# Gate and up projections of a decoder layer: two of eight pairs of channel tiles by seven products of block sums, some low parts by accumulating transfers

## The chip, the cores and the metric

The kernel runs on one core of a Trainium2 chip. The metric is device time in microseconds (us) of one execution; lower is better. The engines of the core are named as in the profile: PE multiplies matrices (PEld is its loading of the stationary operand), DVE and ACT work element by element, POOL does little arithmetic here and issues software DMA transfers, SP issues the weight loads.

## What is computed

One decoder layer over 256 tokens of 2048 channels: a normalised input projection, three branches (windowed attention, pooling, a state-space mixer), an output projection, and a feed-forward part, in which the change lies. All of it is float32.

```
h2 = rmsnorm(x, ln2_w)
gu = h2 @ w_gate_up                     # 2048 x 11264: 5632 gate columns, then 5632 up columns
x = x + (silu(gu[..., :D_FF]) * gu[..., D_FF:]) @ w_down
return rmsnorm(x, final_w)
```

## The kernel before

PE multiplies float32 in a reduced form, so each operand is split in two: `hi`, the value rounded by a cast, and `lo`, what the cast lost. A product is then three matmuls (`three`): x_hi by w_hi, x_hi by w_lo, x_lo by w_hi. The activations are split once. The weights are split as they stream in: `weights` loads 1 MB of a weight matrix (`raw`, 4 channel tiles of 128 rows by 512 columns, on SP's queue) and makes two pieces of it, each of 2 channel tiles, 128 partitions by 1024 elements. For each, `split` has ACT cast `whi` from `raw` and then DVE subtract, `wlo = raw - whi`. There are four buffers of `raw` and five each of `whi` and `wlo`, so that a piece can be made only when the products of the fifth piece before it are done.

The feed-forward part takes the 5632 columns in 11 blocks of 512 (FB = 11), in three parts of 4, 4 and 3 blocks (FF_PARTS), numbered 0 to 10. For a block, `tokens_block` makes the gate (16 channel tiles, 2 tiles of tokens, three matmuls of 128x512 each: 96 matmuls) and then the up projection (96 more), each into two of the four PSUM banks of `acc`. ACT puts the gate through Silu (L871), DVE multiplies the up projection by it (L877). The result `ff` has tokens on its partitions and is wanted with channels there: `turn` makes 16 small transposes on DVE (L342, tile `tt`) and then splits `tt` into `f_hi` (ACT) and `f_lo` (DVE). After each part the down projection takes those `f` tiles as its activations.

The code does not write out the order on each engine. A scheduler sorts the instructions by the order of the program and by what they depend on; each engine then runs its own list strictly in order. `turn` does not run where it is called: it puts its pieces in a list (`later`), and the products call `side` behind each piece of weights, which takes the next entry from that list. So the 16 transposes of a block stand among the weight pieces of the block after it.

Lines of before that the text names: L139 and L140 (the two halves of `split`), L200 to L202 (`three`), L342 (`turn`), L618 (a transfer `mt` of an earlier stage, issued by POOL), L857 (the sum behind the down projection), L862, L871, L877. The same code has other numbers after the change: the split is L142 and L143, `three` is L211 to L213, the transposes are L460.

Of the kernel before, what the change touches and what calls it, by code (L numbers as in the profile page):

```python
# [71 lines left out]
def hybrid_block(ctx: ExitStack, tc: tile.TileContext, ins, out):  # L72
# [6 lines left out]
    small = ctx.enter_context(tc.tile_pool(name="small", bufs=1))  # L79
    dram = ctx.enter_context(tc.tile_pool(name="dram", bufs=1, space=bass.MemoryType.DRAM))  # L80
# [11 lines left out]
    def k1(shape, dt=F32, name="k1", tag="k1", bufs=6):  # L92
        return work.tile([P, *shape], dt, tag=tag, name=name, bufs=bufs)
# [51 lines left out]
    def weights(loads, shape):  # L145

        raw = wpool.tile([P, *shape], F32, tag="raw", name="raw", bufs=4)
        for to, src in loads:
            sp.dma_start(to(raw), src)
        n, cols = shape  # L150
        parts = []
        for h in range(2):
            a, b = h * (n // 2), (h + 1) * (n // 2)
            hi = wpool.tile([P, b - a, cols], F32R, tag="whi", name="whi", bufs=5)
            lo = wpool.tile([P, b - a, cols], F32R, tag="wlo", name="wlo", bufs=5)
            split(raw[:, a:b], hi, lo)
# [264 lines left out]
    v = work.tile([P, T, 256], F32, tag="v", name="v", bufs=1)  # L421
# [220 lines left out]
    bnat = k2([GROUPS, P], F32, "bnat", "bnat", 1)  # L642
# [184 lines left out]


# [19 lines left out]
    fw = [k1([256], F32, "fw", "tk", 16) for _ in range(8)]  # L848
# [16 lines left out]

    for some in FF_PARTS:
        f = Parts(4 * len(some), "f")
        for i, b in enumerate(some):
            a_ = k4([T, NB], F32, "ff")
            for t, a in enumerate(tokens_block(x2p, KD, plain_loads(wgu, 0, b * NB, NB), NB)):  # L870
                act.activation(a_[:, t, :], a, AF.Silu, scale=rstd2[:, t:t + 1])  # L871
# [76 lines left out]
```

## Time and profile before

| | |
|---|---|
| median of 3 runs | 1663.43 us (1662.54 to 1664.08) |
| the profiled execution | 1662.15 us |
| its span, from the first to the last instruction | 1660.4 us |
| what lies around the span | 1.75 us |
| PE busy | 1645.3 us, 99% of the span |
| DVE busy | 1139.6 us, 69% |
| ACT busy | 825.2 us, 50% |
| POOL busy | 65.9 us, 4% |
| mean granted clock of PE | 0.998 of full speed |

An engine is busy, in this table, while it has an instruction in work. Matmuls overlap, so PE's share says only that it nearly always had one in work; the distance between the starts of two matmuls says how fast they pass. A wait is put down to the instruction that released it.

### The profile page before, as it was taken

What the parts mean: (1) busy time and instruction counts of PE and PEld (TensorE: products, weight loads), DVE (VectorE), ACT (ScalarE), POOL (GpSimd) and SP (SyncE); (2) the same over time, 40 slices, a digit from 0 to 9 for tenths busy, and PEclk for the clock granted to TensorE, in tenths of its full rate; (3) what the DMA queues carried; (4) which work ended last, traced back from release to release, by engine and by line L of the source; (5) the groups of instructions that cost most, each with busy time, mean ns of one, the idle gap of its engine ahead of it and who ended that gap; (6) DMA issues with size and microseconds to landing.
All of it is one profiled execution on the core that took longest, in us unless ns stands there. A gap on an engine that the chain in (4) does not pass through costs nothing.

```text
span 1660.4 us, 20066 instructions
## 1 busy us (share of the span) xinstructions
PE 1645.3 (99%) x7815; PEld 1373.5 (83%) x7815; DVE 1139.6 (69%) x1592; ACT 825.2 (50%) x1071; POOL 65.9 (4%) x62
## 2 busy tenths in 40 slices
PE   9999999999999999999999999999999999999997
PEld 8888888888888888888788888888888888888887
DVE  7689898955654569844898866665556666446675
ACT  6467678544444456644445544443344444344443
POOL 1000001200300000000000000000000000000000
PEclk9999999999999999999999999999999999999999
DMA  9654665455566555655575565556655655655552
GB/s 298 185 174 142 186 203 190 171 182 181 189 204 195 187 171 183 228 196 184 178 253 190 186 202 184 183 191 210 201 178 203 202 186 195 201 184 198 194 173 89
DMA packets 185647, 316.68 MB, mean 191 GB/s; under 512 B 7532, under 2 KB 57968, under 8 KB 185552
## 3 DMA queue, kind: packets, MB, share of 16 engines
q1 hardware_dynamic: 183856, 310.67, 56.6%
q0 software_dynamic: 1552, 4.66, 0.9%
q8 instruction: 61, 1.00, 0.2%
q14 instruction: 34, 0.28, 0.0%
q10 hardware_dynamic: 144, 0.07, 0.0%
HBM read 313.25 MB, written 2.13 MB: 190 GB/s over the span
## 4 chain that ended last, share of the span: by engine, by line
PE 94%; DVE 3%; ACT 1%; DMA 1%; issue 0%; POOLq 0%; SPq 0%; POOL 0%; DVEq 0%; ACTq 0%
PE acc L202 26%; PE acc L200 26%; PE acc L201 26%; PE acc L238 9%; PE acc L239 5%; DVE tt L342 2%; DVE wlo L140 1%; PE sm L675 1%; DMA x<-in_x_dram 1%; PE tr L524 0%; ACT whi L139 0%; PE sm L567 0%; PE tr L556 0%; PE sm L682 0%; PE sm L688 0%
## 5 line engine op out<-in xcount | busy, mean ns | idle before, releaser
L140 DVE TENSOR_TENSOR wlo<-raw,whi 128x1024 fp32r<-128x1024 f32 (+2 forms) x582 | 704.6, 1226 | 440.3 <-ACT whi L139 438.6
L139 ACT CAST whi<-raw 128x1024 fp32r<-128x1024 f32 (+2 forms) x582 | 605.5, 1044 | 664.8 <-PE acc L202 595.5
L200 PE MATMUL acc<-whi,x2p_hi 128*128 128x512 f32 x704 | 273.9, 389 | 0.0
L201 PE MATMUL acc<-wlo,x2p_hi 128*128 128x512 f32 x704 | 273.9, 389 | 0.0
L202 PE MATMUL acc<-whi,x2p_lo 128*128 128x512 f32 x704 | 273.9, 389 | 0.0
L238 PE MATMUL acc<-h,whi 128*128 128x512 f32 x672 | 238.4, 398 | 0.0
L200 PE MATMUL acc<-whi,h 128*128 128x512 f32 (+1 forms) x544 | 211.4, 389 | 1.8 <-ACT h L142 1.0
L202 PE MATMUL acc<-whi,h 128*128 128x512 f32 (+1 forms) x544 | 208.6, 385 | 0.3
L201 PE MATMUL acc<-wlo,h 128*128 128x512 f32 (+1 forms) x544 | 208.7, 384 | 0.0
L239 PE MATMUL acc<-h,wlo 128*128 128x256 f32 x672 | 189.0, 282 | 0.0
L201 PEld LDWEIGHTS acc<-wlo,x2p_hi 128*128 128x128 f32 x704 | 132.1, 188 | 27.5
L200 PEld LDWEIGHTS acc<-whi,x2p_hi 128*128 128x128 f32 x704 | 132.1, 188 | 27.4
L202 PEld LDWEIGHTS acc<-whi,x2p_lo 128*128 128x128 f32 x704 | 132.1, 188 | 27.4
L238 PEld LDWEIGHTS acc<-h,whi 128*128 128x128 f32 x672 | 126.0, 188 | 30.3 <-issue 1.8
L202 PE MATMUL acc<-whi,f_lo 128*128 128x512 f32 (+1 forms) x352 | 134.5, 382 | 0.4 <-DVE f_lo L140 0.4
L200 PE MATMUL acc<-whi,f_hi 128*128 128x512 f32 (+1 forms) x352 | 134.4, 382 | 0.0
L201 PE MATMUL acc<-wlo,f_hi 128*128 128x512 f32 (+1 forms) x352 | 134.4, 382 | 0.0
L239 PEld LDWEIGHTS acc<-h,wlo 128*128 128x128 f32 x672 | 126.9, 189 | 1.9 <-issue 1.8
L200 PEld LDWEIGHTS acc<-whi,h 128*128 128x128 f32 x544 | 102.3, 188 | 23.5 <-issue 2.3
L202 PEld LDWEIGHTS acc<-whi,h 128*128 128x128 f32 x544 | 101.9, 188 | 21.2 <-DVE h L143 0.7
L201 PEld LDWEIGHTS acc<-wlo,h 128*128 128x128 f32 x544 | 102.2, 188 | 20.8 <-issue 0.7
L342 DVE STREAM_TRANSPOSE tt<-ff 32x256 f32<-32x256 f32 x176 | 76.7, 436 | 2.7
(238 smaller groups left out, 1744.1 us busy)
## 6 DMA issues: line engine op xcount, KB each, us to landing
raw<-in_w_in_dram SPq DMA_DIRECT2D x106, 1024.0 KB, 5.2
raw<-in_w_gate_up_dram SPq DMA_DIRECT2D x88, 1024.0 KB, 5.1
raw<-in_w_down_dram SPq DMA_DIRECT2D x43, 1024.0 KB, 5.1
raw<-in_w_ssm_br_dram SPq DMA_DIRECT2D x16, 1024.0 KB, 5.1
raw<-in_w_out_dram SPq DMA_DIRECT2D x16, 1024.0 KB, 6.2
raw<-in_w_attn_br_dram SPq DMA_DIRECT2D x8, 1024.0 KB, 5.1
raw<-in_w_pool_br_dram SPq DMA_DIRECT2D x8, 1024.0 KB, 5.0
x<-in_x_dram SPq DMA_DIRECT2D x8, 512.0 KB, 7.9
```

The lines of the kernel that those rows point to most:

```text
L139: act.copy(hi, src)
L140: dve.tensor_tensor(lo, src, hi.bitcast(F32), ALU.subtract)
L200: pe.matmul(o, lhsT=xh, rhs=yh, start=first, stop=False)
L201: pe.matmul(o, lhsT=xh, rhs=yl, start=False, stop=False)
L202: pe.matmul(o, lhsT=xl, rhs=yh, start=False, stop=last)
L238: pe.matmul(accs[c], lhsT=hi[:, j, cols], rhs=a.both(k), start=k == 0, stop=False)
L239: pe.matmul(accs[c][:, :SEQ], lhsT=lo[:, j, cols], rhs=a.hi(k), start=False, stop=k == KD - 1)
L342: dve.transpose(to[32 * j:32 * j + 32, :, :, i, :], src[32 * i:32 * i + 32, :, :, j, :])
L675: pe.matmul(p[:, i * HD:(i + 1) * HD], lhsT=mt[:, i, :], rhs=xdt[:, i, :], start=True, stop=True)
```

## The change

Gate and up of a block are made together, by `two_blocks`, which uses all eight PSUM banks at once: four of `acc` (q1, q7, q5, q6), two of `tr` (q2, q4) and two of `sm` (q3, q8). The 16 channel tiles form eight pairs. For a pair, the activations are two tiles of tokens by two channel tiles, and the weights two channel tiles by two blocks of columns (gate and up): a product of 2 by 2 blocks. Pairs 0 and 1 (`forms`) make it from seven products of sums of blocks, the others from eight products of blocks. The pairs go in the order 0, 2, 1, 3, 4, 5, 6, 7.

- The sums on the activation side are made once (`block_forms`, on DVE). Those on the weight side are made in every block (`block_weights`): `vu` (two blocks), then one sum into `raw` (L278), then another (L279), all on DVE, and each is split. Such a pair has three pieces of two tiles and one of one tile (`shi`, `slo`). Call the three A (the two gate blocks as loaded), B (`vu`) and C (the two later sums): pair 0 makes A, B, C and pair 1 makes A', B', C'. Pair 2 between them has the pieces D and E.
- After pair 1 four merges put sums of the products together (L324 to L328): `s1` by ACT from PSUM, `u2`, `u3`, `s5` and `u2` again by DVE. Behind the last pair DVE adds these to the banks q2, q4 (L994) and q3, q8 (L1001); Silu and the multiplication (L995, L1002) then work on SBUF.
- Pairs 3 and 6 (`by_dma`) get the low part of their weights in another way: ACT writes `lo = -raw` (L161), a transfer issued by POOL (L162) takes `raw` from SBUF and adds it onto `lo` in SBUF (512 KB, accumulating), and ACT casts `hi` (L165). DVE does nothing for these pairs. There are four such transfers in a block, 44 in all. Pair 3's two pieces are called F and G here. `side` is called with 1.8 times the share behind such a piece.
- `raw` has three buffers instead of four; a raw tile of gate and up is filled by two loads of 512 KB. Small tiles of the early stages go to a pool that is closed before this stage.

The core of the diff:

```
-    def weights(loads, shape):
-
-        raw = wpool.tile([P, *shape], F32, tag="raw", name="raw", bufs=4)
+    def weights(loads, shape, by_dma=False):
+        raw = wpool.tile([P, *shape], F32, tag="raw", name="raw", bufs=3)
         for to, src in loads:
             sp.dma_start(to(raw), src)
         n, cols = shape
@@ -153,7 +157,14 @@
             a, b = h * (n // 2), (h + 1) * (n // 2)
             hi = wpool.tile([P, b - a, cols], F32R, tag="whi", name="whi", bufs=5)
             lo = wpool.tile([P, b - a, cols], F32R, tag="wlo", name="wlo", bufs=5)
-            split(raw[:, a:b], hi, lo)
+            if by_dma:
+                act.activation(lo, raw[:, a:b], AF.Copy, scale=-1.0)
+                pool.dma_start(
+                    lo.rearrange("p a c -> p (a c)"), raw[:, a:b].rearrange("p a c -> p (a c)"), accum_op=ALU.add
+                )
+                act.copy(hi, raw[:, a:b])
+            else:
+                split(raw[:, a:b], hi, lo)
             parts.append((a, b, hi, lo))
         return parts
...
+    def block_weights(w, k, c1, c2):
+        raw = wpool.tile([P, 4, NB], F32, tag="raw", name="raw", bufs=3)
+        for j, c in enumerate((c1, c2)):
+            sp.dma_start(raw[:, 2 * j:2 * j + 2, :], rows(w, k, 2, c, NB))
+        vu = wpool.tile([P, 2, NB], F32, tag="vu", name="vu", bufs=2)
+        out = []
+        def part(src):
+            hi = wpool.tile([P, 2, NB], F32R, tag="whi", name="whi", bufs=5)
+            lo = wpool.tile([P, 2, NB], F32R, tag="wlo", name="wlo", bufs=5)
+            split(src, hi, lo)
+            out.extend((hi[:, i], lo[:, i]) for i in range(2))
+        part(raw[:, 0:2])
+        dve.tensor_tensor(vu, raw[:, 0::3], raw[:, 2:3].broadcast_to([P, 2, NB]), ALU.add)
+        part(vu)
+        dve.tensor_tensor(raw[:, 2], vu[:, 0], raw[:, 3], ALU.add)
+        dve.tensor_tensor(raw[:, 0], raw[:, 2], raw[:, 1], ALU.add)
+        part(raw[:, 0::2])
+        hi = late.tile([P, NB], F32R, tag="shi", name="shi", bufs=3)
+        lo = late.tile([P, NB], F32R, tag="slo", name="slo", bufs=3)
+        split(raw[:, 3], hi, lo)
+        out.append((hi, lo))
+        return out
+    def two_blocks(a, forms, w, c1, c2, nk, by_dma=()):
+        q1, q7, q5, q6 = acc(), acc(), acc(), acc()
+        q2, q4, q3, q8 = tr(), tr(), sm(), sm()
+        seven = sorted(forms)
+        plain = [p for p in range(nk // 2) if p not in forms]
+        order = []
+        for i, p in enumerate(seven):
+            order += [p] + plain[i:i + 1]
+        order += plain[len(seven):]
+        for p in order:
+            ka, kb = 2 * p, 2 * p + 1
+            if p in forms:
+                f = forms[p]
+                b11, b21, v, u, z, w_, b22 = block_weights(w, ka, c1, c2)
+                first, last = p == seven[0], p == seven[-1]
+                tok = [slice(t * P, (t + 1) * P) for t in range(T)]
+                def form(i):
+                    return f[:, 0, i], f[:, 1, i]
+                def tile_(k, t):
+                    return a.hi(k)[:, tok[t]], a.lo(k)[:, tok[t]]
+                for q, x, y, ends in (
+                    (q1, tile_(ka, 0), b11, True),
+                    (q7, form(3), u, True),
+                    (q5, form(1), v, True),
+                    (q6, form(2), w_, True),
+                    (q2, tile_(kb, 0), b21, False),
+                    (q4, tile_(kb, 1), z, False),
+                    (q3, form(0), b22, False),
+                ):
+                    three(q, *x, *y, first, last and ends)
+                if last:
+                    s1, u2, u3, s5 = (k2([NB], F32, n) for n in ("s1", "u2", "u3", "s5"))
+                    act.copy(s1, q1)
+                    dve.tensor_tensor(u2, q6, s1, ALU.add)
+                    dve.tensor_tensor(u3, q7, u2, ALU.add)
+                    dve.tensor_tensor(s5, q5, u2, ALU.subtract)
+                    dve.tensor_tensor(u2, q5, u3, ALU.subtract)
+            else:
+                by = p in by_dma
+                loads = [
+                    ((lambda r, j=j: r[:, 2 * j:2 * j + 2, :]), rows(w, ka, 2, c, NB)) for j, c in enumerate((c1, c2))
+                ]
+                for j, (_, _, hi, lo) in enumerate(weights(loads, [4, NB], by)):
+                    for t in range(T):
+                        q = ((q2, q4), (q3, q8))[j][t]
+                        for k in range(2):
+                            xh, xl = a.hi(ka + k)[:, t * P:(t + 1) * P], a.lo(ka + k)[:, t * P:(t + 1) * P]
+                            three(
+                                q, xh, xl, hi[:, k], lo[:, k],
+                                q is q8 and p == plain[0] and k == 0, p == plain[-1] and k == 1,
+                            )
+                    side((1.8 if by else 1.0) * 1024 * SHARE)
+        return ((q2, s1), (q4, u3)), ((q3, s5), (q8, u2))
...
+    forms = block_forms(x2p, (0, 1))
     for some in FF_PARTS:
         f = Parts(4 * len(some), "f")
         for i, b in enumerate(some):
             a_ = k4([T, NB], F32, "ff")
-            for t, a in enumerate(tokens_block(x2p, KD, plain_loads(wgu, 0, b * NB, NB), NB)):
-                act.activation(a_[:, t, :], a, AF.Silu, scale=rstd2[:, t:t + 1])
+            gates, ups = two_blocks(x2p, forms, wgu, b * NB, DFF + b * NB, KD, by_dma=(3, 6))
+            for t, (q, more) in enumerate(gates):
+                dve.tensor_tensor(a_[:, t, :], q, more, ALU.add)
+                act.activation(a_[:, t, :], a_[:, t, :], AF.Silu, scale=rstd2[:, t:t + 1])
             if b == FB - 1:
                 act.activation(tiny([1], "junk1"), a_[:, 1, :1], AF.Square)
                 act.activation(tiny([1], "junk1"), rstd2[:, :1], AF.Sqrt)
-            for t, a in enumerate(tokens_block(x2p, KD, plain_loads(wgu, 0, DFF + b * NB, NB), NB)):
+            for t, (q, more) in enumerate(ups):
+                dve.tensor_tensor(more, q, more, ALU.add)
                 dve.scalar_tensor_tensor(
-                    a_[:, t, :], a, rstd2[:, t:t + 1], a_[:, t, :], ALU.mult, ALU.mult
+                    a_[:, t, :], more, rstd2[:, t:t + 1], a_[:, t, :], ALU.mult, ALU.mult
                 )
             turn(a_, 4 * i, f)
         k0, nk = 4 * some[0], 4 * len(some)
```

What this moves is shown at the border between two blocks. First DVE before the change: `raw_8473` is the last weight tile of a block, `raw_8509` the first of the block behind it.

```order
L140 TENSOR_TENSOR wlo_8476<-raw_8473,whi_8475 128x1024
L140 TENSOR_TENSOR wlo_8480<-raw_8473,whi_8479 128x1024
L877 SCALAR_TENSOR_TENSOR ff_8120<-acc_8279,rs2_r_7781,ff_8120 128x512
L877 SCALAR_TENSOR_TENSOR ff_8120<-acc_8280,rs2_r_7781,ff_8120 128x512
L342 STREAM_TRANSPOSE tt_8419<-ff_8120 32x2x4x32 x16
L140 TENSOR_TENSOR wlo_8512<-raw_8509,whi_8511 128x1024
L140 TENSOR_TENSOR wlo_8516<-raw_8509,whi_8515 128x1024
L140 TENSOR_TENSOR f_lo_7809<-tt_8419,f_hi_7808 128x1024
```

The transposes are followed by two pieces of weights and then by `f_lo`. Next, DVE after the change: `ff_8543` is the result of a block. `raw_8943` (pieces D and E) and `raw_8994` (A', B' and C', with `whi_8998`, `whi_9003` and `whi_9009`) already belong to the block behind it, whose A, B and C stand just ahead of these rows.

```order
L143 TENSOR_TENSOR wlo_8947<-raw_8943,whi_8946 128x1024
L1002 SCALAR_TENSOR_TENSOR ff_8543<-s5_8694,rs2_r_7788,ff_8543 128x512
L1001 TENSOR_TENSOR u2_8692<-sm_8551,u2_8692 128x512
L143 TENSOR_TENSOR wlo_8951<-raw_8943,whi_8950 128x1024
L1002 SCALAR_TENSOR_TENSOR ff_8543<-u2_8692,rs2_r_7788,ff_8543 128x512
L143 TENSOR_TENSOR wlo_8999<-raw_8994,whi_8998 128x1024
L460 STREAM_TRANSPOSE tt_8889<-ff_8543 32x2x4x32 x16
L143 TENSOR_TENSOR wlo_9004<-vu_8997,whi_9003 128x1024
L279 TENSOR_TENSOR raw_8994<-raw_8994 128x512
L143 TENSOR_TENSOR f_lo_7840<-tt_8889,f_hi_7839 128x1024
L143 TENSOR_TENSOR wlo_9010<-raw_8994,whi_9009 128x1024
```

The 16 transposes now stand between the low parts of A' and B'; ahead of them, among D, E and A', are the sums and products that end the block before. L279, from which C' is cast, and `f_lo` come behind B'. On ACT before the change, around the cast `f_hi` of the same block:

```order
L139 CAST whi_8511<-raw_8509 128x1024
L139 CAST whi_8515<-raw_8509 128x1024
L139 CAST whi_8545<-raw_8543 128x1024
L139 CAST f_hi_7808<-tt_8419 128x1024
L139 CAST whi_8549<-raw_8543 128x1024
```

ACT after the change, at the same border; `raw_9047` is pair 3, with the pieces F (`whi_9050`, `wlo_9051`) and G (`whi_9055`, `wlo_9056`):

```order
L142 CAST whi_8998<-raw_8994 128x1024
L142 CAST whi_9003<-vu_8997 128x1024
L142 CAST f_hi_7839<-tt_8889 128x1024
L324 COPY s1_9038<-acc_8891 128x512
L142 CAST whi_9009<-raw_8994 128x1024
L165 CAST whi_9050<-raw_9047 128x1024
L161 ACTIVATE wlo_9051<-raw_9047 128x1024
L161 ACTIVATE wlo_9056<-raw_9047 128x1024
L165 CAST whi_9055<-raw_9047 128x1024
```

`f_hi` and the cast of C' are now ahead of all four operations of pair 3, and the cast of G is the last of them. POOL's transfer onto `wlo_9051` is issued ahead of the one onto `wlo_9056`. On PE, after the change, at the end of C' and the beginning of F and G (`acc`, `tr` and `sm` are banks):

```order
L211 MATMUL tr_8895<-whi_9050,x2p_hi_7109 128x512
L212 MATMUL acc_8894<-wlo_9010,forms_7832 128x512
L213 MATMUL acc_8894<-whi_9009,forms_7832 128x512
L212 MATMUL tr_8896<-wlo_9010,x2p_hi_7107 128x512
L213 MATMUL tr_8896<-whi_9009,x2p_lo_7108 128x512
L211 MATMUL tr_8896<-whi_9050,x2p_hi_7109 128x512
L211 MATMUL sm_8897<-whi_9055,x2p_hi_7109 128x512
L211 MATMUL sm_8898<-whi_9055,x2p_hi_7109 128x512
L212 MATMUL tr_8895<-wlo_9051,x2p_hi_7109 128x512
L213 MATMUL tr_8895<-whi_9050,x2p_lo_7110 128x512
L211 MATMUL tr_8895<-whi_9050,x2p_hi_7109 128x512
```

PE starts F and G with four matmuls that need `whi` alone. The last row but two, L212 of `tr_8895`, is the first to use `wlo_9051`; the other 19 of the 24 matmuls of F and G stand behind it.

## Rows read from the trace of the kernel before

**Rows 1.** The page: busy time by engine, and the chain that ended last.

```profile
PE 1645.3 (99%) x7815; PEld 1373.5 (83%) x7815; DVE 1139.6 (69%) x1592; ACT 825.2 (50%) x1071; POOL 65.9 (4%) x62
...
PE 94%; DVE 3%; ACT 1%; DMA 1%; issue 0%; POOLq 0%; SPq 0%; POOL 0%; DVEq 0%; ACTq 0%
```

**Rows 2.** Windows, two blocks: busy us (instructions) by engine, clock, DMA share, GB/s.

```profile
975.40:1018.90 43.50, 43.50 (x193) 36.04 (x192) 28.57 (x37) 19.13 (x19) 0.00 (x0) 1.00 0.58 194
1018.90:1062.40 43.50, 43.50 (x193) 36.03 (x192) 28.56 (x37) 19.12 (x19) 0.00 (x0) 1.00 0.57 193
```

**Rows 3.** Waits of PE, whole span: total, times, longest.

```profile
PE acc L201 <- DVE wlo L140: 2.3, 2, 2.1
...
PE acc L202 <- DVE f_lo L140: 0.4, 1, 0.4
```

**Rows 4.** Waits between engines for the weight pieces, whole span.

```profile
ACT whi L139 <- PE acc L202: 595.5, 376, 3.5
DVE wlo L140 <- ACT whi L139: 438.6, 327, 3.4
```

**Rows 5.** Timeline of PE in a block: start, duration.

```profile
966.11 0.39 PE L200 MATMUL acc<-whi,x2p_hi 128*128 128x512 f32 x1
966.33 0.39 PE L201 MATMUL acc<-wlo,x2p_hi 128*128 128x512 f32 x1
966.56 0.39 PE L202 MATMUL acc<-whi,x2p_lo 128*128 128x512 f32 x1
966.79 0.39 PE L200 MATMUL acc<-whi,x2p_hi 128*128 128x512 f32 x1
```

**Rows 6.** Timeline of ACT at the border of two blocks; in brackets idle time.

```profile
964.95 1.06 ACT L139 CAST whi<-raw 128x1024 fp32r<-128x1024 f32 x1 [1.66 <-PE acc L202]
...
983.99 1.06 ACT L139 CAST f_hi<-tt 128x1024 fp32r<-128x1024 f32 x1 [1.66 <-DVE tt L342]
984.94 1.06 ACT L139 CAST whi<-raw 128x1024 fp32r<-128x1024 f32 x1
```

**Rows 7.** Timeline of DVE at the same border.

```profile
974.20 1.22 DVE L140 TENSOR_TENSOR wlo<-raw,whi 128x1024 fp32r<-128x1024 f32 x1 [1.49 <-ACT whi L139]
975.34 1.40 DVE L877 SCALAR_TENSOR_TENSOR ff<-acc,rs_r,ff 128x512 f32<-128x512 f32 x2
976.77 7.18 DVE L342 STREAM_TRANSPOSE tt<-ff 32x256 f32<-32x256 f32 x16
983.99 2.36 DVE L140 TENSOR_TENSOR wlo<-raw,whi 128x1024 fp32r<-128x1024 f32 x2
986.26 1.22 DVE L140 TENSOR_TENSOR f_lo<-tt,f_hi 128x1024 fp32r<-128x1024 f32 x1
```

**Rows 8.** Groups by line: three smaller operations.

```profile
L871 ACT ACTIVATE ff<-acc,rs_r 128x512 f32<-128x512 f32 x22 | 15.1, 690 | 9.4 <-PE acc L202 9.4
...
L857 DVE TENSOR_TENSOR x<-acc,x 128x512 f32<-128x512 f32 x22 | 14.2, 684 | 0.7 <-PE acc L202 0.7
...
L862 DVE TENSOR_TENSOR x<-x,fw 128x256 f32<-128x256 f32 x14 | 5.2, 420 | 0.4 <-ACT junk L860 0.2
```

**Rows 9.** POOL transfers of 512 KB: duration of the issue, and landing times.

```profile
L618 POOL DMA_DIRECT2D mt<-upto_rows x8: 530/546/599, 117.3 to 310.2; - x8
...
DMA to landing us min/median/max: 4.0/4.8/7.3
```

**Rows 10.** Weight loads of 1 MB from 978 to 1106 us: landing times.

```profile
DMA to landing us min/median/max: 4.9/5.0/6.2
```

**Rows 11.** The end, in windows of 2 us.

```profile
1650.00:1652.00 2.00, 2.00 (x17) 1.80 (x15) 1.20 (x3) 1.10 (x2) 0.00 (x0) 1.00 0.36 135
1652.00:1654.00 2.00, 0.01 (x1) 0.00 (x0) 1.49 (x7) 0.20 (x1) 0.00 (x0) 1.00 1.03 373
1654.00:1656.00 2.00, 0.00 (x0) 0.00 (x0) 1.50 (x5) 1.12 (x2) 0.00 (x0) 0.83 0.23 83
1656.00:1658.00 2.00, 0.00 (x0) 0.00 (x0) 0.00 (x0) 0.00 (x0) 0.00 (x0) 0.50 1.03 374
```

More of the change, by code (lines that the diff above doesn't have):

```diff
@@ L79, in hybrid_block @@
     small = ctx.enter_context(tc.tile_pool(name="small", bufs=1))
+    early_pool = ExitStack()
+    early = early_pool.enter_context(tc.tile_pool(name="early", bufs=1))
     dram = ctx.enter_context(tc.tile_pool(name="dram", bufs=1, space=bass.MemoryType.DRAM))
@@ L92, in k1 @@
     def k1(shape, dt=F32, name="k1", tag="k1", bufs=6):
-        return work.tile([P, *shape], dt, tag=tag, name=name, bufs=bufs)
+        return early.tile([P, *shape], dt, tag=tag, name=name, bufs=bufs)
     def tiny(shape, name, bufs=2):
@@ L226, in plain_loads, with block_forms @@
         return lambda i, n: [(lambda r: r[:, :, :], rows(w, k0 + i, n, c0, cols))]
+    def block_forms(a, pairs):
+        out = {}
+        for p in pairs:
+            y = k2([2, T, P], F32, "fy")
+            for k in range(2):
+                dve.tensor_tensor(
+                    y[:, k].rearrange("p t s -> p (t s)"),
+                    a.hi(2 * p + k).bitcast(F32), a.lo(2 * p + k).bitcast(F32), ALU.add,
+                )
+            f = k2([4, P], F32, "ff4")
+            dve.tensor_tensor(f[:, 1], y[:, 0, 1], y[:, 1, 1], ALU.subtract)
+            dve.tensor_tensor(f[:, 2], f[:, 1], y[:, 0, 0], ALU.subtract)
+            dve.tensor_tensor(f[:, 0], f[:, 2], y[:, 1, 0], ALU.add)
+            dve.tensor_tensor(f[:, 3], y[:, 0, 0], y[:, 0, 1], ALU.subtract)
+            t = late.tile([P, 2, 4, P], F32R, tag="forms", name="forms", bufs=2)
+            split(f, t[:, 0], t[:, 1])
+            out[p] = t
+        return out
@@ new lines, in block_weights @@
+    def block_weights(w, k, c1, c2):
[19 more added lines that the diff above has]
+        out.append((hi, lo))
+        return out
@@ new lines, in two_blocks @@
+    def two_blocks(a, forms, w, c1, c2, nk, by_dma=()):
[43 more added lines that the diff above has]
+                        q = ((q2, q4), (q3, q8))[j][t]
+                        for k in range(2):
+                            xh, xl = a.hi(ka + k)[:, t * P:(t + 1) * P], a.lo(ka + k)[:, t * P:(t + 1) * P]
+                            three(
+                                q, xh, xl, hi[:, k], lo[:, k],
+                                q is q8 and p == plain[0] and k == 0, p == plain[-1] and k == 1,
+                            )
+                    side((1.8 if by else 1.0) * 1024 * SHARE)
+        return ((q2, s1), (q4, u3)), ((q3, s5), (q8, u2))
@@ L419, in hybrid_block @@
     dve.tensor_copy(rst, rp[:, :SEQ])
-    v = work.tile([P, T, 256], F32, tag="v", name="v", bufs=1)
+    v = early.tile([P, T, 256], F32, tag="v", name="v", bufs=1)
     dt_in = tiny([T, SSM_HEADS], "dt_in", 1)
@@ L639, in mix_product @@
         dve.tensor_tensor(mt, mt, cb.unsqueeze(1).broadcast_to([P, HPG, P]), ALU.mult)
-    bnat = k2([GROUPS, P], F32, "bnat", "bnat", 1)
+    bnat = early.tile([P, GROUPS, P], F32, tag="bnat", name="bnat", bufs=1)
     def b_turn():
@@ L826, in hybrid_block @@
             turn(m4[j], 4 * j, mp)
+    early_pool.close()
+    late = ctx.enter_context(tc.tile_pool(name="late", bufs=1))
     x2 = []
@@ L847, in hybrid_block @@
     wgu, wd = ins["w_gate_up"][0], ins["w_down"][0]
-    fw = [k1([256], F32, "fw", "tk", 16) for _ in range(8)]
+    fw = [late.tile([P, 256], F32, tag="fw", name="fw", bufs=8) for _ in range(8)]
     for i, f_ in enumerate(fw):
@@ L890, in hybrid_block @@
         n = min(8, nk - i)
-        raw = wpool.tile([P, n, 256], F32, tag="raw", name="raw", bufs=4)
+        raw = wpool.tile([P, n, 256], F32, tag="raw", name="raw", bufs=3)
         sp.dma_start(raw, rows(wd, k0 + i, n, 3 * NB + 256, 256))
```

## The prediction

> **What bounds the kernel now.** I read the page first: PE is busy for 99% of the span, and PE is 94% of the chain that ended last [rows 1]. Windows of the length of one block show that the feed-forward part has no hole in it: PE 43.50 of 43.50 us, clock 1.00, while DVE works 28.6 us and ACT 19.1 us of the same time [rows 2]. The waits of PE over the whole span hold only two that concern split operands, 2.3 and 0.4 us [rows 3]. The long waits are those of ACT and DVE: ACT waits 595.5 us for products to end, DVE 438.6 us for ACT [rows 4]. That is the buffer rule at work, since a piece can be cast only when the fifth piece before it is used up. So PE bounds this stage, the engines ahead of it are held back by their buffers and not by their work, and time is gained only if PE has fewer matmuls and still never waits.
>
> The prices I use: matmuls start 0.68 us apart for three, 0.2267 each [rows 5]. ACT casts a piece in 1.06 us, about 0.2 us after the products that free its buffer, and 0.95 apart when two follow each other [rows 6]. DVE makes one low part in 1.22 us, 1.15 apart in a row; reads of a 128x512 PSUM bank take 0.70 each; 16 transposes take 7.18 us [rows 7]. An SBUF sum of 128x512 is half a low part, 0.6; a PSUM sum is 0.65 apart (0.684 long), a 128x256 one 0.42, ACT's read of a PSUM bank 0.69 [rows 8].
>
> **What is removed.** Two pairs in each of 11 blocks lose one product of three matmuls each: 66 matmuls by 0.2267, 15.0 us. A block is 186 matmuls, 42.16 us, in place of 192 and 43.5.
>
> **What is added on PE's way.** I walk through one steady block in time from its first matmul (t = 0), with PE never late, and look for where an operand comes after it is wanted. A piece of pairs 2 to 7 is 12 matmuls, 2.72 us. Pair 0 takes until 4.76, pair 2 (D, E) until 10.2, pair 1 (A', B', C', its short piece) until 14.96, F until 17.68, G until 20.40.
>
> DVE's list around t = 0 is the one in the order above. B's buffer is that of a piece that ends at -8.16 (pair 6's first), so its cast ends at -6.9 and DVE is never free after that: B, vu, C, D, E and A' at 1.15 each, slo and L278 at 0.6, two L994 and two L1001 at 0.65, two L1002 at 0.7 make 12.1 us. So A' is ready at 5.2, where PE wants it near 10.2. Then come the 16 transposes, until 12.45 (with 0.1 of change-over). Only then comes the low part of B', at 13.67, and PE wants it at 11.56 (six matmuls of pair 1 don't need it and stand ahead): **2.1 us late**. Before the change the same transposes hid behind two finished pieces, with DVE idle for a third of the block. Behind B' are L279 (until 14.3), f_lo (15.4) and the low part of C' (16.7), the last 0.3 late.
>
> ACT has the cast of C' behind L279: it ends at 15.4. The in-order list then has F's cast (16.35), F's and G's `lo = -raw` (17.35, 18.3; I price them as casts of the same shape) and G's cast last (19.3). PE's list has four matmuls of F and G that need casts alone, so they end at 19.75. Then F's low part is wanted: ACT finished the negative at 17.35, and the accumulating transfer takes x from there. 20 matmuls (4.53 us) follow until pair 4. Their nominal end is 20.40, so the block loses S = 17.35 + x + 4.53 - 20.40 = **x + 1.5**, the 2.4 above inside it; for however short an x at least 19.75 + 4.53 - 20.40 = 3.9.
>
> No row shows an accumulating transfer. The nearest is `mt`, 512 KB issued by POOL: 4.0, 4.8 in the median, at most 7.3 from issue to landing [rows 9]. Two accumulating transfers run at once here, beside a weight load; 1 MB of those takes 5.0 to 6.2 [rows 10], which is as many bytes as an addition reads. I take x = 5.5, between median and highest, and S = 7.0; the ends are x = 4.0 (S 5.5) and 10, twice `mt`'s median (S 11.5).
>
> The Trainium skill ("DMA: Bandwidth & Descriptors", Anatomy of one DMA — SWDGE (gpsimd) path) fits such a transfer as 2.0 us plus its bytes at 436 GB/s. For 512 KB that is an estimate of 3.2 us, and by it S would be 4.7 and the time 1698; the only rows of that kind say 4.8 in place of 3.2, so I don't take it. The Trainium skill also says ("Collectives: The Full Stack", The bandwidth ceiling) that an addition inside a transfer is slow because it reads two sources. No row here shows that; with the second read at the same rate the estimate is 4.4 us, S 5.9, 1708.
>
> **Where it applies.** Blocks 1, 2, 3, 5, 6, 7, 9 and 10 have the same order at their beginning: 8 by 7.0 is 56. Blocks 4 and 8 come behind a down projection, with no transposes and no sums ahead of them; ACT reaches F's negative by 8.5 and the transfer has 7 us of cover, so 0 (if x were 10, 2 us each). Block 0 has the last transposes of the stage before, and the sums of the activations on DVE (four of 128x256 at 0.42, eight of 128x128 that I put at 0.25, two splits of 128x512 at 0.6: 4.9 us): 11.9, between 8 and 16. At the end of block 10 the added sums make `f_lo` later; it made PE wait 0.4 before [rows 3]; I add 2.
>
> At nothing: the merges behind pair 1, since banks are needed again only a block later and DVE has free time from pair 4 on; pair 6's transfers, since ACT has some 7 us of lead by then; two loads of 512 KB in place of one of 1 MB; three `raw` buffers, since a tile lasts 24 matmuls or 5.4 us, a load 5.0, and two tiles stay ahead (at most 2 us at the start of the kernel). If pair 6's cover were gone too, that is x - 5 in each block.
>
> **Sum**: -15.0 + 56 + 11.9 + 2.0 = +54.9. The profiled execution takes 1662.15 us, its span 1660.4; it would take 1717.1. The median of the runs is 1.3 above the profiled one: **1718 us**.
>
> **The rivals.**
> - The transfers are quick, or PE's order saves it from them, and only the transposes and G's late cast cost: S = 3.9 to 5.5, in all -15.0 + 9 by 3.9 + 4.9 + 2.0 = +27, 1690 to 1705. For it: 512 KB landed in 4.0 once [rows 9]. Against it: these run in pairs.
> - It ends on the other side: nothing is late, because DVE and ACT are further ahead at the border than I have them, and only the 66 matmuls count: 1648. DVE's row of B' would have to stand 2.1 us earlier and F's negative some 7 us earlier. Break-even is at S = 0.9 (nine blocks, and 6.9 besides). For it: DVE idles for a third of the old block [rows 2]. Against it: my count of DVE's work in a new block is 14 low parts (16.5 us), 7.2 of transposes, and 15 of sums and the rest, 39 of 42 us, and what little is free lies at the wrong end of the block, behind the buffers.
> - The transfers take 8 to 10 us, or the gaps cost more than themselves: +75 to +95, 1738 to 1758. My longest gap lies ahead of F's low part, 19.75 to 22.85, 3.1 us. At the end of the trace, PE's clock stands at 1.00 in the 2 us after the last matmul, 0.83 in the next two and 0.50 behind that [rows 11], so such a gap is about where it falls. Each microsecond's work at half clock costs another: with 3 us of matmuls at half clock behind each of 8 gaps, 24 us, 1742. The Trainium skill ("TensorE: Matmul & The Clock Gate", HAM oscillation) says that gaps which return with every tile make PE pay for the low clock again after each; the trace agrees only with the fall itself, at its end.
>
> **How the numbers follow.** A change under 0.2%, 3.3 us, can't be told from none with this kernel. The forecast's case (S 5.5 to 8.8, 1705 to 1734) has 0.42, the quick transfers 0.22, the slow ones or the clock 0.25, the hidden case 0.11, of which 0.08 is faster, 0.03 within 0.2%. All else is slower, 0.89. The range reaches from 1680, below the floor of the second case, to 1762, above x = 10; it leaves out the hidden case and some 0.07 above.
>
> **What would show it.** PE's matmuls fall by 66; PE waits for `wlo` by DVE (B', about 2 us in each of 8 or 9 blocks) and for the accumulating transfer or ACT's cast of G right behind it; blocks 4 and 8 run in 42.2 us, the steady ones in 46 to 54 us; the landing time of L162 is x, 4 to 7.3. Busy time of DVE in a steady block is near 39 us. I am wrong if the steady blocks take 43.5 us or less, if the waits lie elsewhere in the block (at the merges or pair 6), or if `lo` lands late enough that pair 6 stalls as well. A clock under 1.00 in those blocks is the third rival's mark.

## The result, and the profile after

The change makes the kernel slower: 1799.48 us in the median (1797.91 to 1801.65) against 1662.99 beside it, a ratio of 1.0822 with a 95% interval of 1.0809 to 1.0834. The direction was forecast. The size was not: 136.5 us were lost where 54.9 were worked out, and the time lies above the range.

From the page of the changed kernel: busy time by engine, the software queue (packets, MB, share of 16 engines), and the accumulating transfers (KB each, median us to landing).

```profile
PE 1684.2 (94%) x7749; PEld 1381.9 (77%) x7749; DVE 1233.1 (69%) x1760; ACT 898.7 (50%) x1172; POOL 104.1 (6%) x106
...
q0 software_dynamic: 7888, 27.73, 7.3%
...
wlo<-raw POOLq DMA_DIRECT2D x44, 512.0 KB, 8.4
```

PE's work has not grown. It has 66 matmuls fewer than in [rows 1] and a longer busy time, which means that some of them ran slowly; 6% of the span are holes. An accumulating transfer lands after 8.4 us in the median of all 44, not 5.5; those of F, on which PE waits, land after 6.7 to 7.5 us in the eight steady blocks.

Next, windows by block, with the columns of [rows 2]: blocks 1 and 2, then block 4 and block 8, which follow a down projection.

```profile
995.02:1053.03 58.01, 47.71 (x188) 37.46 (x186) 36.19 (x50) 26.16 (x29) 3.45 (x4) 0.91 0.61 181
1053.03:1110.95 57.92, 48.05 (x188) 37.55 (x186) 37.84 (x51) 26.62 (x30) 3.48 (x4) 0.91 0.61 182
...
1255.95:1299.31 43.36, 42.80 (x188) 34.83 (x186) 21.71 (x24) 21.56 (x23) 3.48 (x4) 1.00 0.79 233
...
1560.29:1602.86 42.57, 42.57 (x187) 34.84 (x186) 21.30 (x23) 21.14 (x23) 3.48 (x4) 1.00 0.80 238
```

A steady block (1, 2, 3, 5, 6, 7, 9 and 10 are meant) takes 58.0 us, not 49; PE is busy for 48 of them and its clock is 0.91. Blocks 4 and 8 take 43.4 and 42.6, nearly what 186 matmuls need. By the times at which the parts begin, gate and up of the three parts grew from 174.08, 174.08 and 130.56 us to 234.48, 217.30 and 159.56: 132.6 us. The stage begins 2.3 us later, and 3.0 come at the end. Together that is the 137.9 us by which the span grew.

The waits of PE (total, times, longest) and, behind them, PE's timeline in block 2 from its thirteenth microsecond:

```profile
PE acc L212 <- DVE wlo L143: 53.9, 17, 5.7
PE tr L212 <- DMA wlo<-raw: 38.3, 10, 4.7
```

```profile
1065.81 0.40 PE L211 MATMUL tr<-whi,x2p_hi 128*128 128x512 f32 x1
1071.85 0.80 PE L212 MATMUL acc<-wlo,forms 128*128 128x512 f32 x1 [5.65 <-DVE wlo L143]
1072.44 0.63 PE L213 MATMUL acc<-whi,forms 128*128 128x512 f32 x1
...
1078.21 0.39 PE L211 MATMUL tr<-whi,x2p_hi 128*128 128x512 f32 x1
1078.43 0.63 PE L211 MATMUL sm<-whi,x2p_hi 128*128 128x512 f32 x2
1082.89 0.50 PE L212 MATMUL tr<-wlo,x2p_hi 128*128 128x512 f32 x1 [3.83 <-DMA wlo<-raw]
```

The two waits are the ones that were forecast, on the low part of B' (`acc<-wlo,forms`) and on F's transfer (`tr<-wlo,x2p_hi`). But they are 5.65 and about 4 us, where the walk gave 2.1 and 3.1 (its other 1.8 us of S lay between the two, at C' and at the cast of G, where PE waits for nothing here). Behind the first the matmuls start 0.43 us apart, half speed, for 5 us (so do eight of them behind the second). Windows over the same stretch show the clock itself:

```profile
1053.03:1066.00 12.97, 12.58 (x52) 9.07 (x50) 12.90 (x19) 6.36 (x8) 0.00 (x0) 1.00 0.47 161
1066.00:1072.00 6.00, 0.35 (x2) 0.15 (x1) 5.83 (x13) 1.43 (x2) 0.00 (x0) 0.88 0.00 1
1072.00:1076.00 4.00, 4.00 (x10) 3.17 (x11) 2.76 (x3) 3.62 (x5) 0.27 (x1) 0.50 0.05 8
1076.00:1079.00 3.00, 3.00 (x11) 2.13 (x9) 1.03 (x2) 3.00 (x4) 1.47 (x2) 0.76 0.98 312
1079.00:1083.00 4.00, 0.17 (x2) 0.11 (x2) 3.96 (x6) 1.16 (x2) 0.00 (x0) 1.00 1.09 227
1083.00:1087.00 4.00, 4.00 (x12) 3.17 (x13) 1.07 (x1) 0.49 (x1) 0.00 (x0) 0.66 0.46 71
```

The clock falls to its lower level (0.50, 1.2 GHz) while PE waits at B', stays there after the wait is over, is back when the wait for F begins, and falls again behind that one. By the starts of the matmuls against the usual 0.227 us, some 4.7 us of the block are lost in this way.

Why is B' so late? Four short pieces of the timelines, each with start and duration, from POOL, SP, DVE and ACT around the beginning of block 2 at 1053.03; behind POOL's two transfers stands the landing time of these two:

```profile
1032.64 0.86 POOL L162 DMA_DIRECT2D wlo<-raw  x1 [13.91 <-ACT wlo L161]
1035.32 0.87 POOL L162 DMA_DIRECT2D wlo<-raw  x1 [1.81 <-ACT wlo L161]
```

```profile
DMA to landing us min/median/max: 8.3/8.4/8.5
```

```profile
1043.70 0.88 SPq L153 DMA_DIRECT2D raw<-in_w_gate_up_dram  x2
1044.69 0.91 SPq L265 DMA_DIRECT2D raw<-in_w_gate_up_dram  x2
```

```profile
1052.76 1.23 DVE L276 TENSOR_TENSOR vu<-raw 128x1024 f32<-128x1024 f32 x1 [5.34 <-DMA raw<-in_w_gate_up_dram]
...
1063.37 7.17 DVE L460 STREAM_TRANSPOSE tt<-ff 32x256 f32<-32x256 f32 x16
1070.57 1.23 DVE L143 TENSOR_TENSOR wlo<-vu,whi 128x1024 fp32r<-128x1024 f32 x1
```

```profile
1070.58 1.05 ACT L142 CAST f_hi<-tt 128x1024 fp32r<-128x1024 f32 x1 [10.04 <-DVE tt L460]
...
1074.39 2.00 ACT L161 ACTIVATE wlo<-raw 128x1024 fp32r<-128x1024 f32 x2
```

The second transfer of pair 6 is issued at 1035.32 and lands 8.3 us later, at 1043.6. At 1043.70 SP issues the load of pair 2: with three buffers of `raw` it takes the one that pair 6's transfers were still reading. Over the whole span, weight loads on SP waited for such transfers this long (total, times, longest):

```profile
SPq L153 <- DMA wlo<-raw: 239.3, 27, 13.6
```

Pair 1's load stands behind it in SP's list, at 1044.69. Pair 2's load lands by 1048.7, pair 1's not before 1052.6, and at 1052.76 DVE begins `vu` of pair 1, released by that load after 5.3 us of idle time. From there on DVE is never free, as in the walk, but later: PE wants B' at 1066.2 (the start of its row less its wait), and the transposes end 4.3 us behind that, where the walk has 0.9; F's negative ends 9.2 us behind it, where the walk has 5.8. Both are 3.4 us late.

### The profile page after: what moved, and what is told of

The parts are those of the page before. It is cut to its first block, busy times and chain, and to the rows that moved or that the text cites. A ratio compares the mean times of both kernels' runs of the same rounds, so it can differ in the third digit from the quotient of the medians.

```text
span 1798.3 us, 20545 instructions
## 1 busy us (share of the span) xinstructions
PE 1684.2 (94%) x7749; PEld 1381.9 (77%) x7749; DVE 1233.1 (69%) x1760; ACT 898.7 (50%) x1172; POOL 104.1 (6%) x106
## 5 line engine op out<-in xcount | busy, mean ns | idle before, releaser
L143 DVE TENSOR_TENSOR wlo<-raw,whi 128x1024 fp32r<-128x1024 f32 (+1 forms) x538 | 651.2, 1223 | 379.9 <-ACT whi L142 377.6
L142 ACT CAST whi<-raw 128x1024 fp32r<-128x1024 f32 (+1 forms) x538 | 552.4, 1039 | 538.9 <-PE acc L213 325.1
L212 PE MATMUL acc<-wlo,h 128*128 128x512 f32 (+1 forms) x544 | 208.7, 384 | 0.3 <-DVE wlo L143 0.3
L212 PE MATMUL tr<-wlo,x2p_hi 128*128 128x512 f32 x308 | 131.5, 427 | 39.2 <-DMA wlo<-raw 38.3
L212 PE MATMUL acc<-wlo,f_hi 128*128 128x512 f32 (+1 forms) x352 | 134.5, 382 | 0.0
L213 PE MATMUL tr<-whi,x2p_lo 128*128 128x512 f32 x308 | 129.1, 419 | 0.0
L211 PE MATMUL tr<-whi,x2p_hi 128*128 128x512 f32 x308 | 126.8, 412 | 0.0
L212 PEld LDWEIGHTS acc<-wlo,h 128*128 128x128 f32 x544 | 102.2, 188 | 20.8 <-issue 0.7
L212 PEld LDWEIGHTS tr<-wlo,x2p_hi 128*128 128x128 f32 x308 | 62.7, 204 | 60.8 <-DMA wlo<-raw 43.2
L212 PE MATMUL sm<-wlo,x2p_hi 128*128 128x512 f32 x264 | 105.0, 398 | 0.0
L213 PE MATMUL sm<-whi,x2p_lo 128*128 128x512 f32 x264 | 104.3, 395 | 0.0
L211 PE MATMUL sm<-whi,x2p_hi 128*128 128x512 f32 x264 | 102.7, 395 | 1.1 <-ACT whi L165 1.1
```

The lines of the kernel that those rows point to most:

```text
L142: act.copy(hi, src)
L143: dve.tensor_tensor(lo, src, hi.bitcast(F32), ALU.subtract)
L211: pe.matmul(o, lhsT=xh, rhs=yh, start=first, stop=False)
L212: pe.matmul(o, lhsT=xh, rhs=yl, start=False, stop=False)
L213: pe.matmul(o, lhsT=xl, rhs=yh, start=False, stop=last)
```

## The experiments

The theory after this reading: a steady block loses 15.85 us over its 42.16 (block 1; 15.4 to 16.4 in the eight) by causes that add up. The transposes stand ahead of B' (2.1 us); pair 6's transfers hold a raw buffer, so that pair 1's load is late (3.5 more at B'); F waits for its transfer; and the clock falls behind each long wait. Rivals: DVE has too much work; transfers slow all loads down; the transfers can't be hidden in this pipeline at all. The edits are edits of the changed kernel.

**Without transfers.**

```diff
-two_blocks(x2p, forms, wgu, b * NB, DFF + b * NB, KD, by_dma=(3, 6))
+two_blocks(x2p, forms, wgu, b * NB, DFF + b * NB, KD, by_dma=())
```

> No pair gets its low part by a transfer; DVE makes all of them (by_dma is empty). Theory: a steady block lost 15.9 us because pair 6's transfers (8.4 us) hold a raw buffer, so that pair 1's weights come late (5.65 us of wait at B' in place of the 2.1 that the transposes alone make), because F waits for its transfer (4.3 us), and because PE runs at half clock behind each of these waits (about 5 us). Without transfers only the 2.1 to 3 us at B' are left, too short for the clock to fall: blocks of 44.3 to 45.5 us, 1670 to 1690 us in all. Rival (DVE is the bound, and the transfers relieve it): DVE has 37.5 us of work in a block now and gets 4.6 more, 42.1 of 42.2; low parts come late everywhere, blocks of 47 us or more, 1705 us or more.

Measured: 1688.00 us, 1.0147 (1.0130 to 1.0164). Waits of PE, then windows of blocks 1 and 2 (block 2 ends at 1076.23), then of a stretch of block 2:

```profile
PE acc L212 <- DVE wlo L143: 24.3, 15, 3.6
```

```profile
985.43:1030.12 44.69, 42.97 (x188) 34.76 (x187) 40.31 (x53) 23.57 (x26) 0.00 (x0) 1.00 0.56 185
1030.12:1076.23 46.11, 44.27 (x188) 36.01 (x186) 40.58 (x54) 22.46 (x24) 0.00 (x0) 0.96 0.53 180
```

```profile
1040.00:1043.00 3.00, 2.03 (x9) 1.31 (x7) 2.90 (x7) 0.41 (x1) 0.00 (x0) 1.00 0.00 0
1043.00:1045.00 2.00, 1.13 (x3) 0.93 (x4) 2.00 (x4) 1.62 (x3) 0.00 (x0) 0.81 0.00 0
1045.00:1047.00 2.00, 2.00 (x6) 1.61 (x5) 2.00 (x3) 2.00 (x3) 0.00 (x0) 0.50 0.00 0
1047.00:1049.00 2.00, 2.00 (x8) 1.56 (x8) 1.45 (x3) 2.00 (x3) 0.00 (x0) 0.84 0.30 32
```

The transfers are worth 111 us of the 136, and the time lies in the forecast's range. The wait at B' is now 1.72 in block 1 and 1.84 in block 2 (1.5 to 2.4 in the eight steady blocks), which is the 2.1 of the walk. DVE works 40 us in a block, and yet is late nowhere but there, 0.3 us at C' in three blocks aside. I had called such waits too short for the clock: block 1 agrees, but in block 2 the clock falls behind 1.84 us, and the block takes 46.1 us. It also falls in blocks 3 and 9, behind 2.35 and 2.18 us, but not in blocks 6, 7 and 10, behind 2.11, 1.86 and 2.41. So in this run the length of the wait alone doesn't say whether the clock falls. Blocks 6 and 9, with waits of 2.11 and 2.18 us, take 45.5 and 46.4 us.

**Pair 3 alone, and pair 6 alone**, by `by_dma=(3,)` and `by_dma=(6,)`.

> Only pair 3 (F and G) by transfers. Theory: pair 6's raw buffer is free in time, so the wait at B' falls from 5.65 to about 2.1 us, but the wait for F's transfer stays, and grows, since PE reaches F sooner: both together still x + 1.5, about 9 to 10 us in a block, and about 2.5 us of half clock behind the longer one; 1745 to 1770 us. Rival (the load of the transfers on the DMA engines slows all weight loads): half the transfers, half of all of it, about 1730, with both waits smaller.

> Only pair 6 by transfers. Theory: the wait for F's transfer is gone, the wait at B' stays at 5.65 us with 2.5 us of half clock behind it, because pair 2's load still waits for pair 6's transfers to leave their raw buffer and pair 1's load stands behind it on SP: about 9 us in a block, 1720 to 1740 us. Rival (what makes B' late is DVE alone, by its transposes and sums): the wait at B' is as without transfers at all, and the time is that of the run without transfers within 10 us.

Measured: 1760.35 us, 1.0585 (1.0564 to 1.0606), and 1746.05 us, 1.0499 (1.0478 to 1.0520). Waits of PE with pair 3 alone:

```profile
PE tr L212 <- DMA wlo<-raw: 42.6, 9, 5.1
PE acc L212 <- DVE wlo L143: 24.1, 13, 3.6
PE sm L211 <- ACT whi L165: 9.9, 9, 1.1
```

and with pair 6 alone:

```profile
PE acc L212 <- DVE wlo L143: 49.7, 14, 5.7
PE tr L212 <- DMA wlo<-raw: 7.1, 8, 1.7
```

This separates the two. With pair 3 alone the wait at B' is back at 1.5 to 3.1 us in the steady blocks (the 3.6 is block 0's), the cast of G is late by 1.1 us, as the walk had it (1.5), and F waits 4.5 to 5.1 us. With pair 6 alone F has no transfer to wait for, and B' waits 4.5 to 5.66 again in seven of the eight steady blocks (in block 1, A' waits 3.5), though pair 6 is five pairs away from it: the wait comes by way of the raw buffer. The 7.1 us for transfers there are pair 6's own low parts, late for PE by up to 1.7 us. The first time lies in its range; the second is 6 us above it, its steady blocks taking 50.5 to 54 us, where I had 51. Over the run without transfers, pair 3's cost 72 us and pair 6's 58, of 111 for both: each more than half, at the places named, and not half each with both waits smaller, as a general load on the DMA engines would have it.

**A copy in place of the addition.**

```diff
 pool.dma_start(
-    lo.rearrange(...), raw[:, a:b].rearrange(...), accum_op=ALU.add
+    lo.rearrange(...), raw[:, a:b].rearrange(...)
 )
```

> The transfers of pairs 3 and 6 copy raw in place of adding it, so their low part is raw itself: the subtraction is left out, all else is the same. Theory (the addition is what makes a transfer slow): landing falls from 8.4 us to mt's 4.8 to 5.3, raw buffers come free 3 us earlier, both waits shrink by about 3 us and the clock falls less: blocks of 48 to 51 us, 1715 to 1740 us. Rival (two transfers at once beside weight loads are slow whatever they do): landing stays at 7.5 us or more and the time above 1780.

Measured: 1764.58 us, 1.0611 (1.0583 to 1.0639), between the two forecasts. From its page, and the landing times of its transfers:

```profile
q0 software_dynamic: 7888, 27.73, 4.5%
...
wlo<-raw POOLq DMA_DIRECT2D x44, 512.0 KB, 6.5
```

The queue's share is 4.5% of 16 engines over 1766.7 us where it was 7.3% of 1798.3. Less the 14.9 us of the transfers that the kernel before has too (0.9% of 1660.4), 44 transfers took 64.6 us as copies and 116.4 as additions: 1.47 and 2.64 us of all 16 engines each. So an addition takes 1.8 times the DMA time of a copy, at the same packets and bytes in this row; what it does with that time no row shows. But only 1.9 us of the landing time go with it: copies in this place land after 6.5 us, not after the 4.8 of [rows 9], whose transfers read from DRAM. The rest may be the crowd there, and two rows point that way, though no run varies it alone. Of the eight `mt`, the four that stand alone land after 4.0 to 5.0 us, the four that are issued in pairs after 4.1 to 7.3. And in the run without the seven products below, F's addition is issued 4 us ahead of G's and lands after 4.5 us in the steady blocks, where in the changed kernel the two are issued 1 us apart and F's takes 6.7 to 7.5.

**Four raw buffers**, with the transfers and without. To make room, `vu` has one buffer and the short pieces two.

```diff
-raw = wpool.tile(..., tag="raw", name="raw", bufs=3)
+raw = wpool.tile(..., tag="raw", name="raw", bufs=4)
-vu = wpool.tile([P, 2, NB], F32, tag="vu", name="vu", bufs=2)
+vu = late.tile([P, 2, NB], F32, tag="vu", name="vu", bufs=1)
```

> Four raw buffers in place of three, with all transfers (to make room, vu has one buffer and the short pieces two). Theory: pair 2's load no longer waits for pair 6's transfers, so pair 1's load comes about 3.5 us sooner and the wait at B' falls from 5.65 to 2.1 to 3 us; the wait for F's transfer stays, so the time is like that with pair 3's transfers alone, 1745 to 1775 us. Rival (B' is late because DVE and ACT are behind, whatever the loads do): B' stays above 5 us, 1790 to 1805 us.

> Four raw buffers and no transfers. Theory: the 2.1 us at B' are the transposes' and stay, and only the late loads at some blocks' ends go: 1675 to 1688 us. Rival (three raw buffers are what is left of the loss without transfers): no wait at B', 1665 us or less.

Measured: 1793.47 us, 1.0781 (1.0759 to 1.0802), and 1678.51 us, 1.0090 (1.0075 to 1.0105). The second came within its range. The first forecast missed, and by number its rival was right. The timeline of DVE in block 2, with the low part of E, the transposes, and the low parts of A' and B', shows why:

```profile
1058.24 1.22 DVE L143 TENSOR_TENSOR wlo<-raw,whi 128x1024 fp32r<-128x1024 f32 x1
1059.38 7.18 DVE L460 STREAM_TRANSPOSE tt<-ff 32x256 f32<-32x256 f32 x16
1066.58 1.23 DVE L143 TENSOR_TENSOR wlo<-raw,whi 128x1024 fp32r<-128x1024 f32 x1
1067.73 1.22 DVE L143 TENSOR_TENSOR wlo<-vu,whi 128x1024 fp32r<-128x1024 f32 x1
```

The chain did come sooner: the transposes end 3.8 us after PE's first matmul of pair 1 (1062.75), and in the changed kernel 5.9 us after it (1064.65). But in this version they stand one piece further ahead, before the low part of A', which PE wants 1.1 us before that of B'; it waits there for 4.7 us. Also, with four buffers it is pair 1 itself that takes over the buffer of pair 6, so the late transfer still holds its load. The run is no clean test of the raw buffers, and I don't count it as one; the test is pair 3 alone against pair 6 alone. Without transfers the fourth buffer, with the order and the smaller buffers that come with it, is worth 9.5 us (1688.00 to 1678.51); the wait is at A' there too, 1.2 us.

**The transposes behind pair 1**, with the transfers and without.

```diff
+if i < len(some) - 1:
+    pause(6.0)
 turn(a_, 4 * i, f)
```

> All transfers, three raw buffers, but the 16 transposes of a block are taken from the list later, behind pair 1's pieces (a pause ahead of them in the list, inside a part). Theory: the wait at B' is gone, since 7.2 us of DVE's work leave its way; F's negative is ready about 7 us sooner, at 13.5 us into the block, and with 8.4 us of transfer F's wait is about 4 us and S about 6, with 2.5 us of half clock: blocks of 49 to 52 us, 1715 to 1745 us. Rival (the transposes aren't on the way, the loads and transfers alone are): 1780 us or more.

> No transfers, and the transposes behind pair 1. Theory: with both causes gone nothing in a steady block is late: 42.2 to 43 us for it, what is left is block 0 (about 8 us for the sums of the activations) and 3 us at the end: 1655 to 1672 us. Rival (DVE, at 42 us of work in a block of 42.2, is now the bound): low parts late elsewhere in the block, 1680 us or more.

Measured: 1751.82 us, 1.0530 (1.0509 to 1.0551), and 1681.13 us, 1.0110 (1.0093 to 1.0127). With the transfers, the waits of PE:

```profile
PE tr L212 <- DMA wlo<-raw: 49.9, 10, 5.7
PE acc L212 <- DVE wlo L143: 15.3, 16, 3.6
```

The wait at B' is gone but for at most 1.1 us, as forecast, and 48 us come back, though pair 1's load still waits for pair 6's transfers: at B' the two causes don't simply add up, a late load costs little there once the transposes are out of the way. The wait for F's transfer grew to 5.5 us, where I had put 4, and the time is 7 us above the forecast. Without transfers, the waits are

```profile
PE tr L212 <- DVE wlo L143: 14.0, 9, 3.4
```

and lie behind pair 3 (0.69, 1.82, 2.55 us in blocks 1 to 3). With the transposes taken up there, the low parts behind them are late. The rival was right here: with 40 us of work in a block and five buffers of low parts to work ahead in, DVE was late at either of the two places tried for the transposes.

**The transfers without the seven products.** Forms are left out, all pairs take eight products, and blocks use the four `acc` banks and the other four in turn.

> The transfers without the seven products: all eight pairs by eight products, gate and up together, pairs 3 and 6 by transfers, three raw buffers; blocks use the four acc banks and the two tr with the two sm banks in turn. 192 matmuls a block. Theory (a transfer of 8.4 us does harm only because ACT reaches it late, behind the sums and transposes at a block's border): without block sums ACT writes F's negative as soon as its buffer is free, four pieces or 10.9 us ahead of F, so all but 0 to 2 us of a transfer lie beside matmuls: 1663 to 1695 us. Rival (transfers of this length can't be hidden with five buffers of low parts): 4 us and more at each of pairs 3 and 6, with the clock falling, 1720 us or more.

Measured: 1675.67 us, 1.0076 (1.0062 to 1.0090). Windows of block 5, and PE's waits for transfers in the whole run:

```profile
1244.90:1288.40 43.50, 43.50 (x194) 36.03 (x192) 23.93 (x32) 22.52 (x23) 3.49 (x4) 1.00 0.78 230
```

```profile
PE acc L212 <- DMA wlo<-raw: 6.0, 4, 4.1
```

The time lies in the forecast's range. 44 transfers that land after 7.1 us in the median cost 6.0 us of waits in all, of which 4.1 stand in block 0 (it takes 49.4 us); the block shown has no hole at all. So such transfers can be hidden: pair 6's, which take 8 to 10 us in the steady blocks, make PE wait 0.9 at most. F's are no test of the length, since they land after 4.5 us here. ACT has F's negative done 8.7 us ahead of F in the block shown; in the changed kernel it stands behind the transposes and the cast of C'. This run takes out the sums, the merges and the seven products together, and doesn't say which of them holds ACT up most.

**Towards a faster kernel.** Three versions without transfers, with the transposes behind pair 1 and four raw buffers. The first makes the sums of the activations a stage earlier; the second also gives the block sums to POOL; the third leaves the sums of the activations behind block 0, which makes all its pairs by eight products (so that 60 matmuls are saved, not 66).

```diff
+if j == 0:
+    later(lambda: forms.update(block_forms(x2p, (0, 1))), 1.2)
...
-dve.tensor_tensor(vu, raw[:, 0::3], ...)
+pool.tensor_tensor(vu, raw[:, 0::3], ...)
...
+if b == 1:
+    forms = block_forms(x2p, (0, 1))
```

> No transfers, transposes behind pair 1, four raw buffers, and the sums of the activations made a stage earlier (right after the first quarter of them is there). Theory: block 0 loses 5 us less, and raw loads in time are worth the 9.5 us that they were worth with the transposes in place: 1664 to 1674 us. Rival (DVE's 42 us of work in a block are the bound, whatever comes early): 1676 us or more.

> As the run before, and the three sums of weight blocks for each of the two pairs are made by POOL in place of DVE. Theory (DVE's work is what is left): DVE has 37 us of work in a block, nothing is late, blocks of 42.2 to 42.8 us: 1650 to 1663 us, a version as fast as the kernel before or faster. Rival (POOL takes 1.6 to 1.9 us for a 128x512 sum, so that a pair's three sums take 6 to 7 us one behind the other): B and C come late, 1680 us or more.

> No transfers, transposes behind pair 1, four raw buffers; the first block makes all its pairs by eight products, and the sums of the activations are made behind it, ahead of block 1 (so 64 products fewer... 60 matmuls in place of 66). Theory (what is left over the 15 us saved is block 0 and the stage's start, where the sums of the activations stand on DVE's way): block 0 takes 43.5 us in place of 48.4 and starts 3 us sooner, the other blocks stay at 43.1: 1656 to 1663 us. Rival (the steady blocks and the end are what is left): 1665 us or more.

Measured: 1666.94 us, 1.0028 (1.0016 to 1.0039); 1706.59 us, 1.0260 (1.0243 to 1.0278); 1663.81 us, 1.0005 (0.9996 to 1.0014). The first lies in its range; in the second the rival was right; the third lies 0.8 us above its range and below its rival's. POOL's rows in the second (count, busy us, mean ns):

```profile
L276 POOL TENSOR_TENSOR vu<-raw 128x1024 f32<-128x1024 f32 x22 | 53.5, 2434 | 460.3 <-DMA raw<-in_w_gate_up_dram 349.7 <-DVE wlo L143 110.6
L279 POOL TENSOR_TENSOR raw<-raw 128x512 f32<-128x512 f32 x22 | 42.0, 1911 | 154.3 <-DVE wlo L143 154.3
```

A sum that DVE makes in 1.22 us takes POOL 2.43, and one of 0.68 takes 1.91; PE waited 21.5 us for low parts at `tr` banks there. The third version is as fast as the kernel before, not faster. Its waits of PE are

```profile
PE tr L212 <- DVE wlo L143: 5.5, 7, 2.6
PE acc L212 <- DVE wlo L143: 2.6, 3, 2.1
```

Its gate and up stages take 175.50, 172.94 and 128.74 us, only 1.5 us less than before in sum, and 2.7 come at the start and end. Even a block without any wait, its block 4 from 1195.39 to 1237.88, takes 42.49 us, not 42.16.

## Why the prediction was wrong

**The step that failed** is the list "At nothing", in its items "pair 6's transfers" and "three raw buffers": together they make pair 1's load late, and the wait at B' 5.65 us in place of 2.1. Beside it stands the clock, which was among the rivals and belongs in the sum: some 4.7 us of a steady block.

- *Matmuls saved.* Right: a block without waits takes 42.6 us in place of 43.5, so the seven products do save PE's time, though a quarter less than counted (block 4 without transfers took 42.49, not 42.16).
- *B' late by the transposes, 2.1 us.* Right in place and size where the load was in time: 1.5 to 2.4 us without transfers, 1.5 to 3.1 with pair 3's alone, and 1.1 at most when the transposes were moved. In the changed kernel it was 5.65. The 3.5 us on top are what "at nothing" hid: I looked at whether pair 6's low parts would be late for PE, and at whether two tiles of `raw` are enough for a load of 5 us, but not at how long a transfer keeps its source, 8.3 us from its issue, and which load waits for that; SP's list then held pair 1's load as well. The price that I named for pair 6, x - 5, is for another thing, its own low parts coming late for PE; of that the changed kernel shows 0.56 us, in block 4. That it would be 3.4 with x = 8.4 is chance. The run with pair 6 alone shows the wait at B' without pair 3's transfers. 8 by 3.5 is 28 us.
- *F's transfer.* Right in place. x was mis-sized: 6.7 to 7.5 us for F's in the steady blocks (8.4 in the median of all) against 5.5. The wait itself was 3.5 to 4.65 us against 3.1 in the walk: in block 2 the low part comes 5.3 us later than there, counted from when B' is wanted, but PE, held up at B' and by the clock, comes to it 4.7 us later too. For the same reason it finds the cast of G done, for which the walk had 1.5 us; with pair 3's transfers alone that wait is there, 1.1 us.
- *The clock.* I had it as a rival's price, for the longest gaps, with 3 us at half clock behind each, which no row gave. It is 4.7 us of block 2, behind two waits; eight such blocks would make some 38 us (an estimate from that one block), the largest part of what was missing. Each of the eight has its clock at 0.50 for a part of the time. No run has waits of 4 us and more without the fall, so this share is read from the distances of the matmuls and not from an experiment. The trace of before has no wait on which to see how readily the clock falls; its end [rows 11] was the only row, with 1.00 still granted 2 us after the last matmul, and without transfers the clock fell behind a wait of 1.84 us.
- *The sum.* A steady block: 5.65 at B', 4.2 at F in the mean, 4.7 by the clock in block 2 and 0.3 by the spacing of matmuls make 14.85 of the 15.85 us over 42.16; the rest lies in waits of 0.3 us and the edges of the long ones. The forecast had S = 7.0; eight times the difference is 70.8. Block 0 lost 18.4 and not 11.9, blocks 4 and 8 lost 1.2 and 0.4 and not 0, the stage began 2.3 us late and the end took 3.0 in place of 2.0. All this makes 82 of the 83 us that were missing.
- *The rivals.* The quick transfers and the hidden case are out. The third rival came nearest: its two halves, long transfers and the clock, both happened, on top of a wait that it didn't have.

On the rules weighed: the Trainium skill's fit ("DMA: Bandwidth & Descriptors", Anatomy of one DMA — SWDGE (gpsimd) path) gave an estimate of 3.2 us, and the additions landed after 8.4 in the median, the copies after 6.5; measurement decides. The Trainium skill also has the rule ("Collectives: The Full Stack", The bandwidth ceiling) that an add in a reduction needs two source reads where a copy needs one. The 2.64 against 1.47 us of DMA time are in line with it; no run here shows the reads themselves.

## What to carry to other kernels

A transfer that takes the place of a vector operation holds its source until it lands. Follow that buffer to the next load, and the load to everything behind it on its queue, before pricing the transfer at the time until its result is wanted. A stall of PE costs more than its own length if the clock falls in it or behind it (here 4.7 us beside 9.5 of waits in block 2), so price both; and saved matmuls are worth nothing while the operands that they need in exchange lie on an engine that must run in one unbroken chain at a block's border.

## What was not expected of the hardware

- The clock fell behind a wait of 1.84 us in one block and not behind one of 2.41 us in another, in the run without transfers; it was at 0.50 in the window from 1045 to 1047 us, after the wait had ended.
- The accumulating transfer took 2.64 us of all 16 DMA engines and 0.87 us of POOL to issue, the same transfer as a copy 1.47 and 0.53 us.
